# Where the arguments of the levels' decays are computed: two GpSimd subtractions and one exponential, or one VectorE subtraction and two exponentials

## Chip, core and metric

The kernel runs on one core of a Trainium2 chip. The metric is the device time of one launch in microseconds (us). Engines are named as the profile names them: PE (TensorE matmul), PEld (TensorE weight load), DVE (VectorE), ACT (ScalarE), POOL (GpSimd), SP (SyncE).

## What is computed

The kernel is one transformer block on a sequence of 1024 rows of 1024: a modulated norm, one input projection, sparse attention (a top-k of index scores masks the keys), gated linear attention (GLA), an output projection and a gated feed-forward. The change touches the GLA alone:

```python
def step(S, inp):                       # one chunk of 64 rows, all heads
    qc, kc, vc, gc = inp
    b = jnp.cumsum(gc, axis=2)          # running sum of the log decays
    diff = b[:, :, :, None, :] - b[:, :, None, :, :]
    decay = jnp.exp(jnp.where(tril[None, None, :, :, None], diff, -jnp.inf))
    A = jnp.einsum('bhid,bhjd,bhijd->bhij', qc, kc, decay)
    o = (jnp.einsum('bhij,bhjv->bhiv', A, vc)
         + jnp.einsum('bhid,bhdv->bhiv', qc * jnp.exp(b), S))
    ...
```

## The kernel before

The kernel does not form the three-index `decay`. It takes chunks of 128 rows and splits the triangle of each into seven levels, with half blocks of s = 64, 32, 16, 8, 4, 2 and 1 rows (`LEVELS`). In a block of 2s columns the running sum at column s - 1 is the reference point: the first s columns (keys) are weighted by exp((ref - b)/16), the last s (queries) by exp((b - ref)/16), so that a product of a weighted key and a weighted query carries the right decay. Heads are handled in two pairs, p = 0 and p = 1, with 64 partitions for each head.

`gla_pair(p, ...)` is a generator. At its step n it emits, in this order:

- `masked(n-3)`: two VectorE predicated copies of the products into the triangle `AT` (L819);
- `products(n-2)`: sixteen matmuls in eight groups of two (L810), on the weighted keys and the weighted queries;
- `decayed(n-1)`: four VectorE multiplications of queries by E into `qz` (L799), one GpSimd multiplication of the first halves of E by the keys, in place (L804);
- `decays(n)`: the weights E of level n, a tile of 128x1024 in the ring `gs` of four buffers. Two GpSimd subtractions write the first halves (L790) and the last halves (L791) of all blocks, one ScalarE exponential goes over all of E (L792).

Two more background streams run at the same time: `topk_act` (32 rounds; each has three ScalarE sign passes with a sum, L654, and four small VectorE instructions, L656 to L661) and `topk_dve` (32 rounds; three VectorE counting passes, L625, and two small VectorE instructions, L629 and L631). Main stream are the projections: PE chains of 24 matmuls (L243 to L245, L252 to L254), whose weights are split into two parts by L215, L217, L219 and L220, on POOL, DVE or ACT. After each unit of a projection, `pump` emits one step of a GLA stream where its rate says so, then a round of `topk_act`, then one of `topk_dve`.

`pin()` fixes the order of all PE and of all VectorE instructions of this stretch to the order in which they are emitted. ACT and POOL have no such order: a list scheduler orders their queues at build time, and may place an instruction far ahead of its place in the text. In the trace the POOL subtractions of pair 0's first four levels stand at 153 to 164 us, and those of pair 1's first four at 243 to 257 us, 25 us and 85 us ahead of the multiplications that use them.

Of the kernel before, what the change touches and what calls it, by code (L numbers as in the profile page):

```python
# [14 lines left out]
AF = mybir.ActivationFunctionType  # L15
ALU = mybir.AluOpType

P = 128
# [50 lines left out]
def hymba_block_kernel(  # L69
# [44 lines left out]
    def gs(shape, dt=F32):  # L114
        return g(shape, dt, tag="gs", bufs=NGS)
# [10 lines left out]
    V, A, G, T, S = nc.vector, nc.scalar, nc.gpsimd, nc.tensor, nc.sync  # L126
# [646 lines left out]
    def gla_pair(p, gq, gk, gv, bT):  # L773
# [8 lines left out]
        def decays(lv):  # L782

            s = LEVELS[lv]
            NB = L // (2 * s)
            E = Es[lv] = gs([P, L])
            Ev = E.rearrange("p (a b) -> p a b", b=2 * s)
            bv = bT.rearrange("p (a b) -> p a b", b=2 * s)
            ref = bv[:, :, s - 1:s].to_broadcast([P, NB, s])
            G.tensor_tensor(Ev[:, :, :s], ref, bv[:, :, :s], ALU.subtract)  # L790
            G.tensor_tensor(Ev[:, :, s:], bv[:, :, s:], ref, ALU.subtract)  # L791
            A.activation(E, E, AF.Exp, scale=1.0 / 16)  # L792

        def decayed(lv):
            s, E = LEVELS[lv], Es[lv]
# [29 lines left out]
        for n in range(S1 + 3):  # L825
            if n >= 3:
                masked(n - 3)
            if 2 <= n < S1 + 2:
                products(n - 2)
            if 1 <= n < S1 + 1:  # L830
                decayed(n - 1)
            if n < S1:
                decays(n)
            if n == S1:
                kb = gs([P, L])
                V.tensor_tensor(kb.rearrange("p (a b) -> p a b", b=P),
                                b3[:, :, P - 1:P].to_broadcast([P, NT, P]), b3, ALU.subtract)
                A.activation(kb, kb, AF.Exp, scale=1.0 / 16)
            if n == S1 + 1:

                both = gs([P, L])
                G.tensor_tensor(both, gq, gk, ALU.mult)
                G.tensor_tensor(gk, kb, gk, ALU.mult)
                eb = gs([P, L])
                A.activation(eb, bT, AF.Exp, scale=1.0 / 16)
                G.tensor_tensor(gq, eb, gq, ALU.mult)
            if n == S1 + 2:
                V.tensor_copy(el, eb.rearrange("p (a b) -> p a b", b=P)[:, :, P - 1])
                pd = ps()
                for cc in range(NT):  # L850
                    T.matmul(pd[:, 2 * cc:2 * cc + 2], lhsT=both[:, cc * P:(cc + 1) * P], rhs=hsel,
                             start=True, stop=True)
            yield
# [692 lines left out]
```

## Time and profile before

| | us |
|---|---|
| median of 3 timed runs | 1409.28 (1407.75 to 1411.63) |
| profiled execution | 1407.83 |
| span from its first to its last instruction | 1406.1 |
| PE busy | 1319.4 (94%) |
| DVE busy | 915.8 (65%) |
| ACT busy | 586.4 (42%) |
| POOL busy | 445.8 (32%) |
| L790 and L791, POOL, 28 instructions, 147 to 352 us | 34.1 |
| L792, ACT, 14 exponentials | 14.8 |

Shares of the whole span hide that the stages have different limits. The stretch that matters here is from 150 to about 480 us, where both pairs of the GLA and both top-k streams run beside the projections.

### The profile page before, as it was taken

Reading aid. Unit: us, or ns where it says so; the run is one execution under the profiler, and the core shown is the slowest. Engines: PE = TensorE matmul, PEld = TensorE weight load, DVE = VectorE, ACT = ScalarE, POOL = GpSimd, SP = SyncE. Lnnn points to the kernel's source line nnn. Section 1 sums busy time; section 2 is a strip of 40 time slices with the busy share of each in tenths; the row PEclk is TensorE's granted clock in tenths of the full one; section 3 lists DMA queues with packets and bytes.
Section 4 is the critical chain, followed back from the end, with each engine's and each line's share of the span. In section 5 each row is a group of like instructions: output and inputs, shape, how many; then the busy total and the mean of one; then the engine's idle time right before and its main releaser. Section 6 shows DMA issues by size and latency. Waiting matters only on the chain.

```text
span 1406.1 us, 18387 instructions
## 1 busy us (share of the span) xinstructions
PE 1319.4 (94%) x6979; PEld 1104.1 (79%) x6979; DVE 915.8 (65%) x1525; ACT 586.4 (42%) x1064; POOL 445.8 (32%) x393
## 2 busy tenths in 40 slices
PE   5999989599899998899997999999999999999997
PEld 3777877488788977688886787878888878888886
DVE  3578799758987855875478676654444556576524
ACT  3376655658363235346573333332323325112202
POOL 3560533313310111304222444443444425232101
PEclk9999999799999999999999999999999999999999
DMA  9701010210311344751221233322221346254102
GB/s 267 210 15 31 1 31 30 61 31 16 105 25 38 90 139 149 261 170 31 105 91 53 97 120 120 120 75 90 76 90 64 127 153 223 90 168 150 46 15 105
DMA packets 93630, 136.36 MB, mean 97 GB/s; under 512 B 6403, under 2 KB 72038, under 8 KB 93542
## 3 DMA queue, kind: packets, MB, share of 16 engines
q1 hardware_dynamic: 89576, 121.49, 27.0%
q0 software_dynamic: 3808, 13.64, 3.1%
q8 instruction: 55, 0.90, 0.3%
q14 instruction: 33, 0.27, 0.1%
q10 hardware_dynamic: 158, 0.06, 0.0%
HBM read 111.04 MB, written 24.13 MB: 96 GB/s over the span
## 4 chain that ended last, share of the span: by engine, by line
PE 68%; DVE 16%; issue 5%; DMA 3%; ACT 3%; SPq 2%; POOL 2%; DVEq 0%; ACTq 0%; POOLq 0%
PE pw L1280 5%; PE pw L1281 4%; PE pw L1282 4%; PE ps L1280 4%; PE ps L1282 4%; PE ps L1281 4%; PE pw L1486 3%; PE pw L1487 3%; PE ps L1486 3%; PE ps L1487 3%; PE pw L1488 3%; PE ps L1488 3%; DVE junk_d L625 3%; PE ps L252 2%; PE ps L253 2%
## 5 line engine op out<-in xcount | busy, mean ns | idle before, releaser
L654 ACT ACTIVATE junk_a<-g,Ya 128x1024 int8<-128x1024 f32 (+2 forms) x96 | 99.9, 1041 | 50.5 <-DVE Ya L661 47.8
L252 PE MATMUL ps<-whi,g 128*128 128x256 f32 x384 | 113.1, 295 | 3.3 <-DVE whi L217 1.4
L254 PE MATMUL ps<-wlo,g 128*128 128x256 f32 x384 | 110.5, 288 | 0.7 <-DVE wlo L220 0.7
L253 PE MATMUL ps<-whi,g 128*128 128x256 f32 x384 | 110.5, 288 | 0.0
L1311 POOL TENSOR_TENSOR g<-g,h 128x512 f32<-128x512 f32 x33 | 52.2, 1582 | 138.2 <-issue 54.0
L1452 POOL TENSOR_TENSOR raw<-raw,g 128x1024 f32<-128x1024 f32 x22 | 58.5, 2665 | 110.2 <-DMA raw<-in_w_down_dram 105.3
L245 PE MATMUL ps<-g,wlo 128*128 128x512 f32 x208 | 82.5, 397 | 5.3 <-DVE wlo L220 5.3
L243 PE MATMUL ps<-g,whi 128*128 128x512 f32 x208 | 84.0, 404 | 0.0
L244 PE MATMUL ps<-g,whi 128*128 128x512 f32 x208 | 82.3, 396 | 0.0
L1282 PE MATMUL ps<-g,wlo 128*128 128x512 f32 x192 | 75.7, 394 | 6.3 <-DVE wlo L1273 6.2
L252 PEld LDWEIGHTS ps<-whi,g 128*128 128x128 f32 x384 | 75.6, 197 | 6.4 <-issue 3.5
L1280 PE MATMUL pw<-g,whi 128*128 128x512 f32 x192 | 76.9, 401 | 1.5 <-DVE h L1329 1.5
L1280 PE MATMUL ps<-g,wlo 128*128 128x512 f32 x192 | 75.7, 394 | 0.7 <-ACT g L1185 0.7
L254 PEld LDWEIGHTS ps<-wlo,g 128*128 128x128 f32 x384 | 75.6, 197 | 0.9 <-DVE wlo L220 0.9
L253 PEld LDWEIGHTS ps<-whi,g 128*128 128x128 f32 x384 | 75.7, 197 | 0.0
L1281 PE MATMUL ps<-g,wlo 128*128 128x512 f32 x192 | 75.3, 392 | 0.4 <-DVE g L1186 0.4
L1281 PE MATMUL pw<-g,whi 128*128 128x512 f32 x192 | 74.9, 390 | 0.0
L1282 PE MATMUL pw<-g,whi 128*128 128x512 f32 x192 | 74.8, 389 | 0.0
L625 DVE TENSOR_SCALAR_CACHE_REDUCE junk_d<-g,Zd 128x640 bf16<-128x640 f32 (+5 forms) x96 | 71.4, 744 | 2.4
L1249 POOL TENSOR_TENSOR gs<-raw,raw 128x512 f32<-128x512 f32 x19 | 25.1, 1319 | 119.5 <-DMA raw<-in_w_gate_up_dram 82.6
L1273 DVE TENSOR_TENSOR wlo<-gs,wlo 128x512 fp32r<-128x512 f32 x44 | 39.6, 901 | 29.0 <-ACT wlo L1272 28.5
L1273 DVE TENSOR_TENSOR whi<-gs,whi 128x512 fp32r<-128x512 f32 x44 | 38.7, 879 | 28.8 <-ACT whi L1272 28.3
(408 smaller groups left out, 3871.0 us busy)
## 6 DMA issues: line engine op xcount, KB each, us to landing
raw<-in_w_gate_up_dram SPq DMA_DIRECT2D x42, 512.0 KB, 3.6
g<-in_w_mod_dram SPq DMA_DIRECT2D x24, 512.0 KB, 6.8
raw<-in_w_in_dram SPq DMA_DIRECT2D x24, 512.0 KB, 3.9
whi<-in_w_mod_dram POOLq DMA_DIRECT2D x24, 512.0 KB, 4.7
hid_d<-g SPq DMA_DIRECT2D x22, 512.0 KB, 2.9
raw<-in_w_down_dram SPq DMA_DIRECT2D x22, 512.0 KB, 4.2
gs<-hid_d SPq DMA_DIRECT2D x22, 512.0 KB, 3.4
g<-in_x_dram SPq DMA_DIRECT2D x16, 512.0 KB, 4.5
```

The source lines that it names most:

```text
L243: T.matmul(pt, lhsT=wh, rhs=rh, start=(k == 0), stop=False)
L252: T.matmul(pt, lhsT=rh, rhs=wh, start=(k == 0), stop=False)
L253: T.matmul(pt, lhsT=rl, rhs=wh, start=False, stop=False)
L254: T.matmul(pt, lhsT=rh, rhs=wl, start=False, stop=(k == KC - 1))
L625: V.tensor_scalar(junk_d[:, :W], top[t] if 0 < i < 16 else score[t], Z[:, j:j + 1].bitcast(F32), -float(TOPK), ALU.is_ge, ALU.add, accum_o ...
L654: A.activation(junk_a[:, :W], score[t], AF.Sign, bias=Y[:, j:j + 1].bitcast(F32), accum_out=acc[:, j:j + 1])
L1280: T.matmul(pt, lhsT=w[:, 0, kk, :], rhs=rh, start=(not more and kk == 0), stop=False, skip_group_check=more)
L1281: T.matmul(pt, lhsT=w[:, 0, kk, :], rhs=rl, start=False, stop=False, skip_group_check=more)
L1282: T.matmul(pt, lhsT=w[:, 1, kk, :], rhs=rh, start=False, stop=(kk == 3), skip_group_check=more)
L1486: T.matmul(po[m], lhsT=ah[:, r], rhs=wh[:, cc], start=(f == 0), stop=False)
L1487: T.matmul(po[m], lhsT=al[:, r], rhs=wh[:, cc], start=False, stop=False)
L1488: T.matmul(po[m], lhsT=ah[:, r], rhs=wl[:, cc], start=False, stop=(f == len(cur) - 1))
```

## The change

The subtractions move from GpSimd to VectorE and become one instruction over the whole of E, with b - ref in both halves. The first halves then have the opposite sign, so that the exponential is split into two, with scale -1/16 on the first halves and 1/16 on the last halves.

```diff
             bv = bT.rearrange("p (a b) -> p a b", b=2 * s)
-            ref = bv[:, :, s - 1:s].to_broadcast([P, NB, s])
-            G.tensor_tensor(Ev[:, :, :s], ref, bv[:, :, :s], ALU.subtract)
-            G.tensor_tensor(Ev[:, :, s:], bv[:, :, s:], ref, ALU.subtract)
-            A.activation(E, E, AF.Exp, scale=1.0 / 16)
+            V.tensor_tensor(Ev, bv, bv[:, :, s - 1:s].to_broadcast([P, NB, 2 * s]), ALU.subtract)
+            A.activation(Ev[:, :, :s], Ev[:, :, :s], AF.Exp, scale=-1.0 / 16)
+            A.activation(Ev[:, :, s:], Ev[:, :, s:], AF.Exp, scale=1.0 / 16)
```

## Rows read from the trace of the kernel before

**Rows 1.** The page's 40 slices of 35 us: busy tenths of PE, granted clock in tenths.

```profile
PE   5999989599899998899997999999999999999997
PEclk9999999799999999999999999999999999999999
```

**Rows 2.** Four stretches: length, then busy us (count) by engine, granted clock, DMA.

```profile
167.00:216.00 49.00, 44.01 (x295) 39.62 (x293) 45.65 (x108) 27.29 (x52) 19.13 (x15) 0.97 0.10 28
243.00:279.00 36.00, 20.89 (x93) 17.04 (x91) 30.36 (x73) 23.14 (x39) 13.75 (x13) 0.81 0.19 58
326.00:346.00 20.00, 17.05 (x145) 16.89 (x144) 18.72 (x47) 18.89 (x31) 6.63 (x6) 1.00 0.01 2
346.00:403.00 57.00, 49.18 (x324) 45.69 (x324) 54.23 (x122) 27.86 (x49) 16.49 (x10) 0.91 0.21 65
```

**Rows 3.** Timeline of PE: start, us, instruction, idle time before it and its releaser.

```profile
250.14 0.80 PE L245 MATMUL ps<-g,wlo 128*128 128x512 f32 x1 [5.29 <-DVE wlo L220]
...
279.35 0.77 PE L875 MATMUL pw<-diag,g 64*128 64x128 f32 x2 [6.74 <-DVE diag L888]
...
345.54 1.13 PE L810 MATMUL pw<-h,gs 128*128 128x128 f32 x8 [2.94 <-DVE h L799]
```

**Rows 4.** Groups by line: count, busy us, mean ns, idle before and its releasers.

```profile
L791 POOL TENSOR_TENSOR gs<-g 128x512 f32<-128x512 f32 x14 | 18.0, 1287 | 0.0
L790 POOL TENSOR_TENSOR gs<-g 128x512 f32<-128x512 f32 x14 | 16.1, 1152 | 90.3 <-DVE g L567 52.4 <-PE pw L810 27.7 <-DVE acca L656 10.2
L792 ACT ACTIVATE gs<-gs 128x1024 f32<-128x1024 f32 x14 | 14.8, 1054 | 19.8 <-POOL gs L791 8.7 <-DVE Fa L659 7.0 <-DVE Ya L661 4.1
```

**Rows 5.** Timeline of DVE: a 128x1024 subtraction and the instruction behind it.

```profile
381.81 1.23 DVE L836 TENSOR_TENSOR gs<-g 128x1024 f32<-128x1024 f32 x1
382.95 2.37 DVE L656 TENSOR_TENSOR acca<-acca,need 128x3 f32<-128x3 f32 x1
```

**Rows 6.** Timeline of DVE: one free group (178.66); the others beside POOL's subtractions.

```profile
150.17 8.85 DVE L567 SCALAR_TENSOR_TENSOR g<-gs,wcol,g 128x1024 f32<-128x1024 f32 x5
...
178.66 1.73 DVE L799 TENSOR_TENSOR h<-g,gs 64x256 f32<-64x256 f32 x4
...
183.45 0.82 DVE L629 TENSOR_SCALAR md<-acc 128x3 int32<-128x3 f32 x1
...
200.73 4.31 DVE L799 TENSOR_TENSOR h<-g,gs 64x256 f32<-64x256 f32 x4
...
243.25 1.05 DVE L657 TENSOR_SCALAR ma<-acca 128x3 int32<-128x3 int32 x1
...
253.70 1.03 DVE L661 SCALAR_TENSOR_TENSOR Ya<-ma,Ya 128x3 int32<-128x3 int32 x1
...
339.12 1.20 DVE L631 SCALAR_TENSOR_TENSOR Zd<-md,Zd 128x3 int32<-128x3 int32 x1
...
342.87 4.14 DVE L799 TENSOR_TENSOR h<-g,gs 64x256 f32<-64x256 f32 x4
```

**Rows 7.** Timelines of ACT (two rows) and DVE: the top-k's wait for its sign passes.

```profile
163.09 0.56 ACT L337 COPY g<-ps 128x512 f32<-128x512 f32 x1
...
164.70 1.04 ACT L792 ACTIVATE gs<-gs 128x1024 f32<-128x1024 f32 x1
...
167.86 0.16 DVE L656 TENSOR_TENSOR acca<-acca,need 128x3 f32<-128x3 f32 x1 [7.74 <-ACT junk_a L654]
...
260.48 0.16 DVE L656 TENSOR_TENSOR acca<-acca,need 128x3 f32<-128x3 f32 x1 [3.02 <-ACT junk_a L654]
```

**Rows 8.** All instructions of a line: duration ns min/median/max, first and last start.

```profile
L804 POOL TENSOR_TENSOR gs<-gs,g x14: 1266/1290/2187, 168.4 to 352.5; 128x512 f32<-128x512 f32 x14
L625 DVE TENSOR_SCALAR_CACHE_REDUCE junk_d<-g,Zd x96: 611/746/876, 170.1 to 428.4; 128x640 bf16<-128x640 f32 x17, 128x512 bf16<-128x512 f32 x17, 128x384 bf16<-128x384 f32 x17, 128x640 bf16<-128x640 bf16 x15
```

**Rows 9.** Timeline of DVE ahead of pair 1's first levels.

```profile
318.85 0.16 DVE L656 TENSOR_TENSOR acca<-acca,need 128x3 f32<-128x3 f32 x1 [0.80 <-ACT junk_a L654]
...
324.88 0.16 DVE L656 TENSOR_TENSOR acca<-acca,need 128x3 f32<-128x3 f32 x1 [1.08 <-ACT junk_a L654]
```

## Prediction

> **What bounds the kernel now.** I read the slices first. PE is nearly full throughout, and where it is not, between 140 and 420 us, its clock dips too: the eighth slice has PE at 5 and the clock at 7 [rows 1]. That is where both pairs of the GLA run. Then the busy time by stretch. From 167 to 216 us PE lacks 5.0 us (49.00 - 44.01), from 243 to 279 us 15.1, from 326 to 346 us 2.95 and from 346 to 403 us 7.8 [rows 2]: 31 us of idle PE. DVE is 93 to 95% busy in three of the four. Between these stretches, at 216 to 243 and from 279 to 326 us, PE hardly waits. Last, what ended PE's idle times: the three long ones, 5.29, 6.74 and 2.94 us, all ended with a DVE instruction, and these are a weight split, a copy of the GLA's state and the weighted queries [rows 3]. They are late only because DVE's order is fixed and each stands behind rounds of the two top-k streams. So in these four stretches DVE's one long queue sets the end, and a microsecond more or less in it goes to the end nearly whole. Elsewhere PE does, and DVE's time is free.
>
> **What the change adds to DVE.** Fourteen subtractions of 128x1024. The row nearest to one is the kernel's own subtraction with a broadcast operand of that size: it takes 1.23 us, and the next starts 1.14 us after it [rows 5]. 14 x 1.14 = 16.0. The place is fixed by the pin: behind `decayed(n-1)`, ahead of the round of `topk_act`. Pair 0's seven stand at about 173 to 215 us, all in the full queue. Of pair 1's, the first levels meet DVE waits of 0.80 and 1.08 us [rows 9], which hide 1.9. Added to the path: 16.0 - 1.9 = +14.1. The two ends are 0 hidden and four levels hidden (+16.0 and +11.4).
>
> **What it takes from POOL, and by that from DVE.** POOL loses 28 instructions, 34.1 us [rows 4]. POOL is not on the path and its own time is worth nothing. But DVE is held up while they run. A free group of four L799 takes 1.73 us; beside POOL's subtractions one took 4.31 and another 4.14. Three-element instructions, 0.16 to 0.17 us when free, took 0.82 to 1.20 us [rows 6]. I went through all DVE instructions from 140 to 480 us that took over 0.15 us more than the same form when free, and put each excess to the POOL instruction whose span covers its start. L790 and L791 own 15.4 us in twenty of them:
> - 150 to 160 us, 2.8, in the five L567 that took 8.85 us together and the instruction behind them [rows 6]. Worth nothing: DVE then waits 7.74 us anyway [rows 7];
> - 183 to 205 us, 4.6 (from the row at 183.45 to that at 200.73, whose excess of 2.6 is 1.1 due to L804);
> - 243 to 247 us, 2.5 (three like the row at 243.25);
> - 252 to 255 us, 1.65 (two, the last at 253.70);
> - 338 to 347 us, 3.75 (0.4, 1.04 at 339.12, 0.87, and 1.5 of the 2.4 in the group at 342.87) [rows 6].
> Off the path: -12.5.
>
> **What moves with it: L804.** Fourteen multiplications on POOL stay, 1.29 us each [rows 8]. Today they cost DVE 10.0 us by the same count. Each will now follow its own subtraction by one exponential, and behind most subtractions stand four small instructions (0.7 us), then three L625 (2.2 us), which no POOL instruction lengthened: their longest is 0.876 us, the free time of the 640-column form [rows 8]. So many of them will meet nothing. Ends: none meets DVE (-10), or all do at today's 1.1 for each that does (+5.4). I take -4, between the middle and the end that the order on DVE speaks for. The Trainium skill says why L625 is left alone (SBUF — State Buffer, section "Who interferes with whom"): VectorE and GpSimd share one port pair, an instruction of VectorE with two SBUF inputs locks against a GpSimd instruction that reads SBUF, whoever comes first holds it for the whole instruction, and a `tensor_scalar` that writes out its accumulator is not among the takers. The rows agree with it on L567, L799 and L625. Taken as strict it would make this term about -8 and the sum -8.8; it would also let the new subtraction, with two SBUF inputs, hold up L804.
>
> **What moves on ACT.** The exponential of 1.05 us [rows 4] becomes two of half the columns. No row has that form; the ends are 0.53 (half of 1.05) and 1.05 each, and the nearest 128x512 instruction is the copy of 0.56 [rows 7]; I take 0.6, so 1.2 a level, 2 us more in all. ACT has that much free (27 of 49 us busy from 167 to 216 [rows 2]). The order counts more. Today the exponential of pair 0's fourth level stands between sign passes of the first round, 164.70, and DVE waits for that round [rows 7]; gone, that is -1.0. I don't count the whole wait of 7.74: the passes stand behind the copy at 163.09, which waits for PE's matmuls, and that copy stays where it is [rows 7]. Likewise two of pair 1's exponentials, run early, delay the round before 260.48 (a wait of 3.02); gone, I take -1.9, since DVE arrives 1.65 us earlier and the round needs its 3.2 us (from the end of the copy, 163.65, to 167.86, less the exponential [rows 7]). Sum -2.9.
>
> **The new wait.** E(n) must now pass DVE, then ACT, before `decayed(n)` on DVE; POOL used to be up to 85 us ahead. A subtraction waits for its buffer of E (PE's products four levels back, over 10 us earlier) and so does not hold DVE. `decayed(n)` waits for the last half's exponential. Between the two stand one round of each top-k stream (3.6 us) at most levels, and a split and a predicated copy (2.4 us) at the tightest, against 1.2 for both exponentials and 0.2 for the signals. If one sign pass (a third of the 3.2) gets in between, 2.5. What is queued behind a late `decayed(n)` is the whole of DVE's order, and PE's products. I take +1.5 for all levels; the ends are 0 and 7 (0.5 a level).
>
> **Clock.** From 243 to 279 us the granted clock averaged 0.81, part of it at the lower level, right behind the idle time of 5.29 us [rows 2, 3]. With shorter gaps PE may keep the upper one. At full clock its 20.89 us would be 16.9, so the ends are 0 and -4; DVE sets that stretch, so I take -1.
>
> **Sum.** 14.1 - 12.5 - 4 - 2.9 + 1.5 - 1 = -4.8 us. The profiled execution took 1407.83 us, of which 1.7 lie outside its span of 1406.1; it is 1.45 below the median of 1409.28. All terms are differences inside the span, so I set the sum against the median: 1409.28 - 4.8 = 1404.5. By stage: pair 0 gains about 7, mostly after 243 us, where only the removals lie; pair 1 loses about 2, as its seven subtractions (less 1.9) and seven instead of three L804 come into a stretch that gives back 3.75.
>
> **Rivals.** (1) A wash, 1409 (1405 to 1413). DVE's relief at 243 to 279 us only lets it run into ACT's loop: a round of sign passes takes ACT 3.2 us, and DVE already waits for it in places (0.80, 1.08 and 3.02 us [rows 7, 9]). Then half of pair 0's gain goes, and L804 meets DVE as often as today. For it: ACT's passes are serial. Against it: ACT idles 22 of 49 us from 167 to 216. Worked out: -4.8 + 3 + 2 = 0 or so, 1409.3.
> (2) Slower, 1418. ACT's queue is filled at build time. If an exponential stands there ahead of the round of sign passes that could have run before it, ACT waits for DVE's subtraction, and DVE then waits for the exponentials and the passes: 1.2 + 3.2 = 4.4 us a level. From a second such level on the gain is gone; with three it is -4.8 + 13.2 = +8.4, 1418. For it: today's queue has exponentials between passes [rows 7], and DVE waited 3.02 us for that. Against it: the passes of a round depend on the round before, which is ahead of the subtraction on DVE by 5 us or more, so that they are ready first. A held-up L804 (the longest today took 2.19 us, free ones 1.27 [rows 8]) would come on top, since late weighted keys hold PE's products.
> (3) A larger gain, 1397. If the first round's passes come ahead of the copy at 163.09, the wait of 7.74 shrinks by up to 6.4 us, and L804 meets DVE nowhere: -4.8 - 3 - 4 = -12. Against it: two queue orders must fall right.
> That the subtraction does not stay in its place on DVE is excluded by the pin.
>
> **Chances.** Forecast (1401 to 1407.5) 0.45, (1) 0.28, (2) 0.19, (3) 0.08. The forecast holds two thirds of its weight below 1405.05, which is 0.3% (4.2 us) under the median, about what a measurement of this kernel can tell from no change. Faster: 0.30 + 0.05 of (1) + 0.08 + a little from the unknown bounds = 0.46. Slower: 0.17 of (2) and 0.04 of (1), 0.21. Same: 0.33. The range for 8 in 10 leaves out most of (2)'s upper half and (3)'s lower: 1396.5 to 1416.
>
> **What would show it.** DVE busy from 150 to 410 us about unchanged although it has 14 instructions more; no instruction of 0.17 us lengthened to 0.8 to 1.2 at 243 to 255 us; PE's gap at 250 us about half, that at 279 us under 4 us; L804 beside L625 most of the time. Wrong, if L799 shows new idle time ahead of it released by ACT, if L656 waits for L654 more often than in the places shown, or if the new subtraction takes more than 1.25 us.

## The result, and the profile after

| | before | after |
|---|---|---|
| median | 1408.51 us (1407.00 to 1411.63, 4 runs) | 1399.18 us (1398.80 to 1401.24, 4 runs) |
| ratio | | 0.9932, 95% interval 0.9920 to 0.9944 |
| profiled execution, span | 1407.83, 1406.1 us | 1398.97, 1397.2 us |

The change takes 9.3 us (0.68%) off, where the forecast was 4.8. The direction was right and the size was half: the time lies below the forecast's own 1401 to 1407.5 us and inside its range for 8 in 10, 1396.5 to 1416. In what follows, "before" and "after" stand for the two kernels. How the gain came about is in good part not what the forecast said, as the stages show.

The page of after: busy time by engine, then PE and its granted clock in 40 slices, to set beside [rows 1].

```profile
PE 1308.9 (94%) x6979; PEld 1095.5 (78%) x6979; DVE 906.9 (65%) x1539; ACT 588.3 (42%) x1078; POOL 413.8 (30%) x365
...
PE   5899999797799998899998999999999999999997
...
PEclk9999999899999999999999999999999999999999
```

DVE has 14 instructions more and is busy 8.9 us less (915.8 before): what it no longer loses beside GpSimd is more than what it got. PE's idle time over the span is not smaller: 1406.1 - 1319.4 = 86.7 us before, 1397.2 - 1308.9 = 88.3 after. PE's busy time is 10.5 us smaller with the same 6979 matmuls. So a look at PE's idle time alone would have found nothing; the stretches have to be looked at one by one, and at the clock.

Three stretches of before, then the same three of after (length, busy us and count by engine, granted clock, DMA):

```profile
150.00:235.00 85.00, 80.01 (x483) 70.55 (x482) 73.75 (x145) 51.32 (x83) 39.78 (x27) 0.98 0.09 26
235.00:326.00 91.00, 75.54 (x467) 65.85 (x466) 64.34 (x176) 52.99 (x119) 27.14 (x20) 0.89 0.14 41
326.00:403.00 77.00, 66.23 (x467) 62.59 (x466) 72.95 (x168) 46.75 (x79) 23.12 (x15) 0.93 0.16 49
```

```profile
150.00:235.00 85.00, 85.00 (x530) 75.72 (x529) 77.83 (x173) 55.73 (x97) 22.28 (x14) 1.00 0.09 26
235.00:326.00 91.00, 78.66 (x553) 70.50 (x551) 62.83 (x189) 60.12 (x133) 16.34 (x11) 0.94 0.14 42
326.00:403.00 77.00, 60.77 (x396) 55.85 (x397) 71.28 (x164) 44.37 (x80) 22.93 (x11) 0.91 0.18 55
```

In the first stretch PE is now full, 85.00 of 85.00 us at full clock. In the second it does 553 matmuls instead of 467. In the third it does fewer, 396 instead of 467, partly since other work has moved into these times. What is lost there is clearer from pairing. PE's order is pinned and the same in both kernels, so the n-th matmul of one is the n-th of the other; the difference of their starts says how far after is ahead (negative) at that piece of work. At these times of the kernel before:

| work at, us | 150 | 200 | 220 to 240 | 280 | 340 | 400 | 420 to 480 | 1350 |
|---|---|---|---|---|---|---|---|---|
| after, us | -1.5 | -6.3 | -9.4 | -18.9 | -19.3 | -11.4 | -11.1 | -8.9 |

Up to 240 us, where pair 0 runs, 7.9 us are gained (the 1.5 us at 150 us lie ahead of the change's work; the kernels below are there between 0.2 us behind and 2.9 us ahead, so this is scatter between executions). Two kernels below that leave pair 0 as it was (pair 1 alone, and pair 1 later on GpSimd) gain 1.2 us in this stretch too, so about that much of the 7.9 belongs to the one profiled execution of before. From 240 to 280 us another 9.5 us follow, where only the removal of pair 1's early GpSimd work lies. Where pair 1 itself runs, 340 to 420 us, 8.2 us are lost. Behind it 2 us more go, in work that the change does not touch.

### The profile page after: what moved, and what is told of

The parts are those of the page before. It is cut to its first block, busy times and chain, and to the rows that moved or that the text cites. A ratio compares the mean times of both kernels' runs of the same rounds, so it can differ in the third digit from the quotient of the medians.

```text
span 1397.2 us, 18382 instructions
## 1 busy us (share of the span) xinstructions
PE 1308.9 (94%) x6979; PEld 1095.5 (78%) x6979; DVE 906.9 (65%) x1539; ACT 588.3 (42%) x1078; POOL 413.8 (30%) x365
## 4 chain that ended last, share of the span: by engine, by line
PE 63%; DVE 18%; issue 5%; ACT 5%; DMA 3%; POOL 3%; SPq 2%; DVEq 0%; POOLq 0%; ACTq 0%
PE pw L1279 5%; PE pw L1280 4%; PE pw L1281 4%; PE ps L1279 4%; PE ps L1281 4%; PE ps L1280 4%; DVE junk_d L625 3%; PE ps L1486 3%; PE ps L1485 3%; PE ps L1487 3%; PE pw L1486 3%; PE pw L1487 3%; PE pw L1485 3%; ACT junk_a L654 2%; DVE h L798 2%
## 5 line engine op out<-in xcount | busy, mean ns | idle before, releaser
L654 ACT ACTIVATE junk_a<-g,Ya 128x1024 int8<-128x1024 f32 (+2 forms) x96 | 99.9, 1041 | 36.2 <-DVE Ya L661 30.4
L252 PE MATMUL ps<-whi,g 128*128 128x256 f32 x384 | 111.5, 290 | 0.0
L253 PE MATMUL ps<-whi,g 128*128 128x256 f32 x384 | 109.1, 284 | 0.0
L252 PEld LDWEIGHTS ps<-whi,g 128*128 128x128 f32 x384 | 74.2, 193 | 2.7 <-issue 2.0
L253 PEld LDWEIGHTS ps<-whi,g 128*128 128x128 f32 x384 | 74.2, 193 | 0.0
L625 DVE TENSOR_SCALAR_CACHE_REDUCE junk_d<-g,Zd 128x640 bf16<-128x640 f32 (+5 forms) x96 | 71.4, 744 | 2.4
```

The source lines that it names most:

```text
L252: T.matmul(pt, lhsT=rh, rhs=wh, start=(k == 0), stop=False)
L253: T.matmul(pt, lhsT=rl, rhs=wh, start=False, stop=False)
L625: V.tensor_scalar(junk_d[:, :W], top[t] if 0 < i < 16 else score[t], Z[:, j:j + 1].bitcast(F32), -float(TOPK), ALU.is_ge, ALU.add, accum_o ...
L654: A.activation(junk_a[:, :W], score[t], AF.Sign, bias=Y[:, j:j + 1].bitcast(F32), accum_out=acc[:, j:j + 1])
```

## Experiments

The questions: which pair brings the gain; whether it is the head start of the first top-k round, the freed VectorE, or merely the order on ACT; what the added subtractions cost; and whether engine, form or place of the subtractions matters. The expectations name the theories as they stood before each kernel ran. "Ahead" is the paired lead over the kernel before, as in the table above; times are medians, with the ratio to the kernel before and its interval.

### One pair at a time

The changed three lines stand under a condition, the old four lines in the other branch:

```diff
+            if p == 0:                     # e2_pair1: p == 1
                 V.tensor_tensor(Ev, bv, bv[:, :, s - 1:s].to_broadcast([P, NB, 2 * s]), ALU.subtract)
```

Pair 0 alone:

> Only pair 0's subtractions move to VectorE; pair 1's stay on GpSimd, two instructions and one exponential a level. Theory A (the gain of the change is pair 0's: ScalarE's queue no longer waits for GpSimd ahead of the first top-k round, about 6.7 us, and pair 1's own stretch only loses, about 8 us): 1398 to 1402 us, the first round's L656 near 160 us, and no loss behind 300 us; what stays of before is the damage that pair 1's early instructions do at 243 to 257 us. Theory B (the gain is VectorE's relief from the shared port alone, equal in kind for both pairs): seven subtractions cost 8 us and give back 4.6 to 7.5, so 1408 to 1411 us.

1400.65 us, 0.9949 (0.9934 to 0.9964). It is 0.6 us ahead at 150 us, 8.5 at 220, 9.6 at 280 and still 9.6 at 480.

Pair 1 alone:

> Only pair 1's subtractions move to VectorE. Theory A: the first round of the top-k starts as late as before (near 168 us), 243 to 279 us gains 8 to 10 us since pair 1's early GpSimd subtractions and exponentials are gone from there, and the stretch from 305 to 400 us loses 7 to 9: 1405 to 1410 us. Theory B: 1404 to 1407 us with no stretch that loses over 3 us.

1408.98 us, 1.0008 (0.9991 to 1.0025). It is 2.7 us ahead at 240 us, 10.9 at 280, 10.3 at 340, 1.9 at 400 and 3.6 at 480. So the two halves do different things: pair 0's is worth 7 us and keeps them; pair 1's gains 8.2 us between 240 and 280 us and loses 8.4 of its own between 340 and 400, 6.7 if 480 is taken for the end. By the medians it is a wash.

### Only the order on ACT

On the kernel before, pair 0's exponentials are queued behind the last sign pass of the first top-k round, so that nothing stands ahead of that round (`first_round[0]` is that pass). GpSimd keeps the subtractions.

```diff
-            A.activation(E, E, AF.Exp, scale=1.0 / 16)
+            with tc.issue_after(first_round[0].ins) if p == 0 else nullcontext():
+                A.activation(E, E, AF.Exp, scale=1.0 / 16)
```

> The kernel before, with one change in ScalarE's queue: pair 0's exponentials are issued behind the last sign pass of the first top-k round. All subtractions stay on GpSimd. Theory A: the first round's L656 comes at 160 to 163 us and not at 168, and 5 to 7 us of it last to the end: 1401 to 1405 us. Theory B: VectorE's lock decides, which this leaves as it is: 1407 to 1410 us.

1407.74 us, 0.9994 (0.9982 to 1.0006): nothing. Its trace shows why. First ACT in the kernel before (start, us, instruction, idle time before it and its releaser; the copy and the exponential of [rows 7] lie between the last two lines and behind them):

```profile
155.99 1.06 ACT L792 ACTIVATE gs<-gs 128x1024 f32<-128x1024 f32 x1 [1.15 <-POOL gs L791]
160.00 1.06 ACT L792 ACTIVATE gs<-gs 128x1024 f32<-128x1024 f32 x1 [2.95 <-POOL gs L791]
162.12 1.06 ACT L792 ACTIVATE gs<-gs 128x1024 f32<-128x1024 f32 x1 [1.06 <-POOL gs L791]
...
163.55 1.15 ACT L654 ACTIVATE junk_a<-g,Ya 128x1024 int8<-128x1024 f32 x1
```

and in after:

```profile
155.90 1.15 ACT L654 ACTIVATE junk_a<-g,Ya 128x1024 int8<-128x1024 f32 x1 [3.82 <-DVE g L568]
...
157.05 0.57 ACT L337 COPY g<-ps 128x512 f32<-128x512 f32 x1
157.52 1.04 ACT L654 ACTIVATE junk_a<-g,Ya 128x896 int8<-128x896 f32 x1
```

The first sign pass needs DVE's L568. In before it is built into ACT's queue behind three exponentials, which wait for GpSimd, and starts at 163.55, though L568 ended at 160.1. In after it starts as L568 releases it. The DVE side, after first and then the reordered kernel:

```profile
148.71 6.83 DVE L567 SCALAR_TENSOR_TENSOR g<-gs,wcol,g 128x1024 f32<-128x1024 f32 x5
...
159.74 0.16 DVE L656 TENSOR_TENSOR acca<-acca,need 128x3 f32<-128x3 f32 x1 [3.88 <-ACT junk_a L654]
```

```profile
149.56 8.86 DVE L567 SCALAR_TENSOR_TENSOR g<-gs,wcol,g 128x1024 f32<-128x1024 f32 x5
158.45 1.05 DVE L568 TENSOR_TENSOR g<-g,dmin 128x128 f32<-128x128 f32 x1
163.38 0.24 DVE L660 TENSOR_TENSOR acca<-acca,need 128x3 f32<-128x3 f32 x1 [3.88 <-ACT junk_a L656]
163.65 0.99 DVE L661 TENSOR_SCALAR ma<-acca 128x3 int32<-128x3 int32 x1
```

The new order alone brings the first round's wait from 7.74 [rows 7] to the same 3.88 us as in after, and its first small instruction from 167.86 to 163.38. But L567 is still held up beside GpSimd (8.86 against 6.83 for five), and GpSimd's work now meets the first rounds, whose small instructions take 1 us instead of 0.17. By the third round 0.5 us of the 4.5 is left. So the head start did not last while GpSimd's work on the same levels stayed beside DVE.

### Engine or form

The kernel after with its one subtraction on GpSimd: the change's form without its engine.

```diff
-            V.tensor_tensor(Ev, bv, bv[:, :, s - 1:s].to_broadcast([P, NB, 2 * s]), ALU.subtract)
+            G.tensor_tensor(Ev, bv, bv[:, :, s - 1:s].to_broadcast([P, NB, 2 * s]), ALU.subtract)
```

> The kernel after with its one subtraction of 128x1024 on GpSimd instead of VectorE, so the form of the change (one subtraction, two exponentials of opposite scale) without the change of engine. Theory A (the engine is the point: GpSimd's work in the first round of the top-k stays the same in time, about 2.1 us a level by two rows of 1.04): within 3 us of the kernel before, 1404 to 1411 us, and the first round's VectorE wait for the sign passes over 6 us as in the kernel before. Theory B (fewer and other instructions are the point): most of the change's gain is there, 1398 to 1403 us.

1411.14 us, 1.0016 (1.0003 to 1.0028). All instructions of the line (duration ns min/median/max), and DVE beside the first four of them:

```profile
L789 POOL TENSOR_TENSOR gs<-g x14: 1892/1958/2122, 153.1 to 351.3; 128x1024 f32<-128x1024 f32 x14
```

```profile
150.35 11.99 DVE L567 SCALAR_TENSOR_TENSOR g<-gs,wcol,g 128x1024 f32<-128x1024 f32 x5
...
167.71 0.16 DVE L656 TENSOR_TENSOR acca<-acca,need 128x3 f32<-128x3 f32 x1 [5.04 <-ACT junk_a L654]
```

One GpSimd instruction takes about as long as the two (1.96 us), holds L567 up more (11.99 us for five), and the first round is as late as before. So the change's form without its engine does not pay; the old form on VectorE was not tried. That the wait is 5.04 us and not over 6, as expected, is because DVE itself comes later by 2.5 us.

### Which of pair 0's levels

The same condition as above, with `p == 0 and lv < 4` and with `p == 0 and lv >= 4`.

> Only the first four levels of pair 0 move to VectorE, those whose GpSimd subtractions ran ahead of the first top-k round. Theory A (most of pair 0's gain is that early bundle, on GpSimd, on the port and in ScalarE's queue): the first L656 at 160 to 161 us, 4 to 8 us gained by 220 us, 1401 to 1405 us. Theory B (the relief at 183 to 205 us, levels 4 to 6, carries it): under 3 us gained by 220 us, 1405 to 1408 us.

1404.84 us, 0.9979 (0.9968 to 0.9990).

> Only the last three levels of pair 0 move to VectorE. Theory A: the first L656 stays near 167 us; 4.6 us of VectorE's waits go, 3.4 us of subtractions come: 0 to 2 us gained by 220 us, 1406 to 1409 us. Theory B: 4 to 7 us gained by 220 us, 1401 to 1404 us.

1404.76 us, 0.9982 (0.9972 to 0.9991). The first four levels are 5.8 us ahead at 200 us and 4.7 at 220; the last three, 1.6 and 4.6. Each gives about half of pair 0's 8.5 us (by the ratios 3.0 and 2.5 us, where pair 0 alone has 7.2). The last three's time lies between the two that were expected. My theory, that the head start at the first levels makes pair 0's gain, is only half right: the last three levels have no head start and gain as much, in the stretch from 183 to 205 us where [rows 6] has GpSimd holding DVE up.

### What the added subtractions cost

The kernel after with the subtraction cut to one column. It leaves the subtraction out: the exponentials read the running sum itself.

```diff
-            V.tensor_tensor(Ev, bv, bv[:, :, s - 1:s].to_broadcast([P, NB, 2 * s]), ALU.subtract)
-            A.activation(Ev[:, :, :s], Ev[:, :, :s], AF.Exp, scale=-1.0 / 16)
-            A.activation(Ev[:, :, s:], Ev[:, :, s:], AF.Exp, scale=1.0 / 16)
+            V.tensor_tensor(E[:, 0:1], bT[:, 0:1], bT[:, 0:1], ALU.subtract)
+            A.activation(Ev[:, :, :s], bv[:, :, :s], AF.Exp, scale=1.0 / 16)
+            A.activation(Ev[:, :, s:], bv[:, :, s:], AF.Exp, scale=1.0 / 16)
```

> The changed kernel with the VectorE subtraction cut to one column, so that its order and its waits stay; the exponentials read the running sums themselves, which leaves the subtraction out. VectorE loses 14 x 1.06 = 14.8 us. If VectorE's queue is the bound in both pairs' stretches, 10 to 14 us come off: 1385 to 1390 us, and the loss from 305 to 400 us shrinks from 8 to about 2. If the loss there comes from ScalarE's queue order and not from VectorE's load, 1391 to 1396 us with the loss there still over 5.

1398.34 us, 0.9940 (0.9920 to 0.9959), no different from after within the intervals, and slower than either expected range (1385 to 1390, 1391 to 1396). And the kernel after with each of pair 0's subtractions done twice:

```diff
+            for _ in range(2 if p == 0 else 1):
                 V.tensor_tensor(Ev, bv, bv[:, :, s - 1:s].to_broadcast([P, NB, 2 * s]), ALU.subtract)
```

> The changed kernel with each of pair 0's seven subtractions done twice on VectorE, 8.0 us more. If VectorE's queue is the bound in pair 0's stretch, 7 to 9 us slower than the changed kernel: 1406 to 1408 us. If PE is the bound there by now and VectorE has a lead of some us, as the run with one-column subtractions makes likely (it took 7.4 us out of that stretch and gained nothing by 300 us), 0 to 5 us slower: 1399 to 1404 us.

1410.90 us, 1.0024 (1.0011 to 1.0038). Against after that is some 12 us for 8 us of DVE work, and slower than either expected range. By the pairing it turns the lead at 220 us from 9.4 us ahead to 3.9 behind. The stretch from 150 to 235 us, first with the short subtraction and then with the doubled one:

```profile
150.00:235.00 85.00, 85.00 (x530) 75.64 (x528) 71.88 (x170) 55.68 (x96) 23.11 (x14) 1.00 0.09 26
```

```profile
150.00:235.00 85.00, 78.12 (x465) 67.87 (x464) 77.85 (x158) 51.49 (x88) 17.94 (x13) 0.94 0.08 26
```

With the short one DVE is busy 6 us less than in after, and PE does the same 530 matmuls: it was full already. What DVE saves, it waits: 1.62 us twice for ACT's passes and 2.88 us for PE, where after has no such waits. With the doubled one DVE is as busy as in after (77.85 and 77.83), it just gets less far, and PE does 65 matmuls fewer, at a clock of 0.94. So after stands at the crossing of two limits in pair 0's stretch: less DVE work buys nothing, more of it is paid in full, and above its price when PE falls idle and its clock falls as well. PE's longest gap there stands ahead of L759, whose operand DVE writes; in the kernel before it was 0.55 us:

```profile
213.47 3.75 PE L759 MATMUL pw<-g,wg 16*128 16x512 f32 x4 [5.14 <-DVE g L819]
```

In pair 1's stretch the short subtraction does help: this kernel is 18.6 us ahead at 340 us and 17.4 at 480, so it loses 1.2 us there where after loses 8.2. So by one execution of each kernel 7.0 us of pair 1's loss are the seven subtractions on a DVE that sets the end (7 x 1.14 = 8.0 in the forecast's terms). The medians do not confirm it: the whole kernel is only 1 us faster than after by the medians, although its profiled execution is 6.3 us ahead at 480 us. Why is not settled. That execution took 1394.86, the fastest of its four, 3.5 us under their median, and 4.1 us of its lead go behind 480 us.

### Another place on GpSimd

If pair 1's gain at 240 to 280 us comes only from GpSimd's early work being gone there, it needs no DVE. In the first kernel pair 0 goes as in after and pair 1 stays on GpSimd, its subtractions queued behind GpSimd's last weight split; in the second one pair 0 stays on GpSimd too, where it was.

```diff
+            if p == 0:
                 V.tensor_tensor(Ev, bv, bv[:, :, s - 1:s].to_broadcast([P, NB, 2 * s]), ALU.subtract)
...
+            else:
+                ref = bv[:, :, s - 1:s].to_broadcast([P, NB, s])
+                with tc.issue_after(last_split[0].ins):
+                    G.tensor_tensor(Ev[:, :, :s], ref, bv[:, :, :s], ALU.subtract)
+                    G.tensor_tensor(Ev[:, :, s:], bv[:, :, s:], ref, ALU.subtract)
+                A.activation(E, E, AF.Exp, scale=1.0 / 16)
```

> Pair 0's subtractions on VectorE as in the changed kernel; pair 1's stay on GpSimd, but are queued there behind the last weight split that GpSimd does ahead of them, so that they stand near 265 to 310 us, where PE is the bound. Theory A (pair 1's early GpSimd instructions at 243 to 257 us cost pair 0's stretch 8 to 9 us, its VectorE subtractions cost its own stretch 7 to 8, and each is needed for neither): matmuls near 300 us come 17 to 19 us earlier than before, and no more than 2 us of that are lost by 420 us: 1389 to 1393 us. Theory B (the two are the price of the work wherever it stands): 1398 to 1402 us, as with pair 0 alone.

1392.07 us (1390.73 to 1396.93, 5 runs), 0.9899 (0.9882 to 0.9917), faster than after, whose interval (0.9920 to 0.9944) lies wholly above this one. GpSimd's timeline:

```profile
258.28 5.00 POOL L221 TENSOR_TENSOR wlo<-raw,whi 128x1024 fp32r<-128x1024 f32 x2 [29.42 <-DVE whi L218]
263.22 1.06 POOL L799 TENSOR_TENSOR gs<-g 128x512 f32<-128x512 f32 x1
264.22 1.08 POOL L800 TENSOR_TENSOR gs<-g 128x512 f32<-128x512 f32 x1
```

> The kernel before with one thing changed: pair 1's GpSimd subtractions are queued behind the last GpSimd split of a weight instead of where they stood, at 243 to 255 us. Pair 0 is as before, nothing is on VectorE. Theory A (pair 1's early GpSimd work and the exponentials behind it cost some 8 us between 243 and 279 us, and their place is what costs, not their engine): the difference of e5_mix and e1_pair0, 8.6 us, comes off the kernel before, 1397 to 1402 us, and the lead of 7 to 10 us appears between 240 and 280 us of the trace and stays. Theory B (it pays only together with pair 0's move): 1405 to 1409 us.

1403.39 us, 0.9959 (0.9942 to 0.9976). Ahead by:

| work at, us | 240 | 280 | 340 | 480 | 1350 |
|---|---|---|---|---|---|
| pair 0 on DVE, pair 1 later on GpSimd | -10.7 | -20.3 | -17.5 | -17.8 | -17.1 |
| pair 1 later on GpSimd, nothing else | -1.8 | -10.0 | -7.3 | -7.7 | -4.8 |

Three kernels, pair 1 on DVE and pair 1 later on GpSimd with and without pair 0, gain 8.2, 9.5 and 8.2 us from 240 to 280 us. What they share is that the subtractions, and the exponentials behind them, are gone from 243 to 257 us, and with them the multiplications at 261 us. So the old place cost 8 to 9 us, and both other places that were tried cure it. Which part weighs how much was not tried; the rows of before and after give 4.1 us of DVE's instructions that the subtractions lengthened, 2.2 that the multiplications did, and 2.1 less of DVE's waits for ACT (3.02 and 1.29 us in before, 1.21 and 0.96 in after). But only the later place on GpSimd keeps it: some 3 us are lost around 310 us and nothing at 340 to 480, where pair 1 on DVE loses 8. GpSimd's subtractions still lengthen DVE's instructions there, by 7.1 us in the first kernel by the forecast's count, but no more than those 3 us show in PE's matmuls. In the last kernel 5.8 us by the ratio is left, between the two theories' times. The trace has the lead of theory A; 2.9 us of it go behind 480 us.

The parts add up: pair 0 on DVE (-7.2 by its ratio) and pair 1 later (-5.8) are -13.0, and both together measured -14.2.

## Why the prediction was right in sign and half in size

The changed instructions in after (duration ns min/median/max, first and last start):

```profile
L789 DVE TENSOR_TENSOR gs<-g x14: 1218/1225/1227, 165.9 to 357.4; 128x1024 f32<-128x1024 f32 x14
...
L790 ACT ACTIVATE gs<-gs x14: 629/632/670, 167.2 to 358.7; 128x512 f32<-128x512 f32 x14
...
L791 ACT ACTIVATE gs<-gs x14: 612/616/672, 167.7 to 359.3; 128x512 f32<-128x512 f32 x14
...
L803 POOL TENSOR_TENSOR gs<-gs,g x14: 1271/1347/3700, 167.9 to 359.4; 128x512 f32<-128x512 f32 x14
```

**Prices.** The subtraction takes 1.22 us, 1.13 to 1.15 to the next instruction; the forecast had 1.23 and 1.14. The half exponentials take 0.61 to 0.63, forecast 0.6. The Trainium skill (ScalarE: Activation LUTs, section "What ACT_TABLE_LOAD costs") gives 186 ns and 0.833 ns an element for an activation with immediate scale and bias, by which an estimate is 186 + 512 x 0.833 = 613 ns. The rows agree (medians of 616 and 632 ns).

**"A microsecond more or less in DVE's queue goes to the end nearly whole", and by that +14.1.** The price holds, up to a limit that the forecast did not have. An estimate by stage from the rows of both traces (the subtractions at 1.14 us, what GpSimd lengthens on DVE by the forecast's count, DVE's waits for ACT) makes DVE's queue 7.5 us shorter up to 240 us, 8.4 shorter from 240 to 280 and 8.8 longer behind it; the pairing has 7.9, 9.5 and 8.2. So both pairs' subtractions were paid nearly in full. Nothing of the 1.9 was hidden: the waits of 0.80 and 1.08 us are there in after too, ahead of pair 1's first subtraction. The limit is PE. In pair 0's stretch it had 85.00 - 80.01 = 4.99 us of idle time to give back, and gave all of it: PE is full there in after. With 2.9 us less PE time for the same 481 matmuls, by the pairing, that makes the 7.9 us gained. Past this, less DVE time buys nothing, as the short subtraction showed; more of it is paid, as the doubled one showed. So the sum needed a cap there: PE's idle time and what its matmuls can save. The change just reached it, and the cap is not what made the gain larger than forecast.

**-12.5 for GpSimd's lengthening of DVE.** The mechanism held: of the 15.4 us due to L790 and L791 nothing is left, and no small instruction of DVE between 243 and 255 us is longer than 0.17. Its ledger was wrong at one place: the 2.8 us at L567 and L568, "worth nothing" because DVE waits 7.74 us anyway, are on the path once that wait shrinks, since ACT's first pass is released by L568.

**-4 for L804.** It measured -7.0 us: the multiplications (L803 in after) now lengthen four DVE instructions by 3.0 in all, where it was nine by 10.0. Ten of the fourteen lengthen nothing. L625 still takes 611 to 875 ns. The rule of the Trainium skill (SBUF — State Buffer, section "Who interferes with whom") that a `tensor_scalar` that writes out its accumulator is not among the takers was the better guide here (about -8 by the forecast's estimate).

**-2.9 for ACT's order.** This is the step that failed most. The failed reading is the copy at 163.09 [rows 7]. I took it to wait for PE's matmuls, and the passes behind it with it. It followed the exponential ahead of it in ACT's queue without a gap, and the exponentials waited for GpSimd; in after, with PE 1.5 us ahead, the same copy runs at 157.05. The first round came 8.1 us earlier: 1.5 was there already, 2.8 is L567 and L568, and 3.9 is the wait, 7.74 to 3.88. So -1.0 should have been -6.7 with the 2.8. This is the third rival's mechanism, which I gave 0.08; its time (1397) was nearer than the forecast's. Order alone did not pay, as the reordered kernel shows.

**+1.5 for the new wait.** L798 (L799 in before) waited for ACT once, 1.5 us. The second rival's mechanism, an exponential ahead of a sign pass, came once in pair 1. ACT and then DVE in after:

```profile
321.29 0.63 ACT L790 ACTIVATE gs<-gs 128x512 f32<-128x512 f32 x1 [1.78 <-DVE gs L789]
...
322.34 0.92 ACT L654 ACTIVATE junk_a<-g,Ya 128x768 int8<-128x768 f32 x1
```

```profile
320.02 1.23 DVE L789 TENSOR_TENSOR gs<-g 128x1024 f32<-128x1024 f32 x1
323.39 0.90 DVE L656 TENSOR_TENSOR acca<-acca,need 128x3 f32<-128x3 f32 x1 [2.13 <-ACT junk_a L654]
...
361.55 1.77 DVE L629 TENSOR_SCALAR md<-acc 128x3 int32<-128x3 f32 x1
363.36 2.27 DVE L631 SCALAR_TENSOR_TENSOR Zd<-md,Zd 128x3 int32<-128x3 int32 x1
```

ACT waited 1.78 us for the subtraction with a ready pass behind it, and DVE 2.13 us for that pass. That is one level, half of what the rival's price of 4.4 said; it did not come a second time. In all, DVE's waits for ACT in the work from 280 to 420 us grew from 5.3 to 8.6 us, where the forecast had 1.5 for all levels. The last two rows are DVE beside GpSimd's L220 and L841, 3.7 us more than their free times together. Meetings of DVE with GpSimd's other work, which no term of the forecast has, cost 2.9 us more in the same work than in before.

**-1 for the clock.** From 150 to 480 us the stretches at the lower level, 1.2 GHz, add up to 34.1 us before and 23.9 after. At half speed 10.2 us of them are worth up to 5 us, which is a bound, since PE also idles in them. From 235 to 326 us the granted clock went from 0.89 to 0.94. The forecast's ends were 0 and -4. The stretch that it spoke of came out at the far end: the 91 matmuls from 243 to 279 us took PE 20.8 us in before and 17.0 in after.

**By stage.** Pair 0 was to gain 7, mostly after 243 us. It gained 7.9 before 240, and the removals after it 9.5. Pair 1 was to lose 2; it lost 8.2. That two errors of 6 to 8 us partly cancel is luck: the total lies nearer to the forecast than its parts. In the forecast's terms, as measured: +16.0 for the subtractions, -15.4 and -7.0 for what GpSimd's subtractions and multiplications no longer lengthen, +2.0 for its other work beside DVE and -2.7 for DVE's waits for ACT make an estimate of -7.1 us. The pairing has -9.6 from 150 to 480 us; the rest is of the size of what PE's matmuls saved, and was not separated further.

**The signs named.** DVE's busy time about unchanged: 211.04 and 211.94 us from 150 to 403. PE's gaps in after (those over 1.5 us from 200 to 400 us):

```profile
237.17 0.50 PE L245 MATMUL ps<-g,wlo 128*128 128x512 f32 x1 [1.68 <-DVE wlo L220]
...
260.43 0.77 PE L874 MATMUL pw<-diag,g 64*128 64x128 f32 x2 [7.50 <-DVE diag L887]
...
330.18 3.12 PE L809 MATMUL pw<-h,gs 128*128 128x128 f32 x13 [6.88 <-DVE h L798]
...
341.32 1.35 PE L809 MATMUL pw<-h,gs 128*128 128x128 f32 x10 [1.71 <-DVE h L798]
...
356.61 0.57 PE L809 MATMUL pw<-h,gs 128*128 128x128 f32 x3 [2.96 <-DVE h L798]
...
368.87 1.41 PE L809 MATMUL pw<-h,gs 128*128 128x128 f32 x5 [7.38 <-DVE h L798]
```

The gap at 250 us [rows 3] shrank from 5.29 to 1.68, more than half. The one at 279 was to fall under 4 and grew from 6.74 to 7.50; it is the same work, 18.9 us earlier. The first rival is not the reason: DVE's waits for ACT's passes on the way there got shorter (1.21 and 0.96 us, from 3.02 and 1.29). PE's idle time over those 91 matmuls fell from 15.5 to 9.6 us in all, and PE now waits for most of it at one place. One sign of being wrong came, the idle time ahead of L799 that ACT released (1.5 us, once); L656 waited more than 0.2 us for L654 in 10 places, as before. The two gaps ahead of L809 at 330 and 369 us show pair 1's loss: PE waits for weighted queries behind DVE's longer order.

**Left open.** 2 us of after's lead, and 2 to 5 us of that of several other kernels, go between 480 and 1350 us, in work that no kernel touches. PE's idle time there is the same in before and after, 22.53 us, and its matmuls take the 2.2 us more. The lower clock takes up 6.8 us there in before and in the kernel with pair 0 on DVE and pair 1 later on GpSimd, and their matmuls take 847.6 and 847.8 us; it takes 10.2 or 13.7 us in after and all others, and their matmuls take 849.5 to 852.2. Whether that is chance was not tried.

## What to carry to other kernels

Work of an idle engine is not free: look at what its instructions lengthen on the engine that sets the end, and at which queue they hold through an instruction that waits for them. Before taking such relief at its full size, cap it stage by stage with the idle time of the engine that would bound next, and what its own work can save (here 4.99 and 2.9 us). Where two halves of a change lie in different stages, try each alone and then another place for the one that doesn't pay: here that made 1392 us of 1399.

## What the runs showed of the hardware that was not expected

- A held-up DVE and a held-up GpSimd cost each other: GpSimd's subtraction of 128x512 takes 1.04 us alone and up to 2.07 beside L567, whose five take 6.83 us without it, 8.85 beside two levels' subtractions in two instructions each, and 11.99 beside three levels' in one each: 1.0 and 1.7 us a level. The Trainium skill (SBUF — State Buffer, section "Who interferes with whom") has the rule that an instruction of VectorE with two SBUF inputs locks against a GpSimd instruction that reads SBUF; the rows agree, and show that the longer GpSimd instruction was the worse neighbour for the same work.
- The new subtraction has two SBUF inputs, and none of the fourteen was lengthened (1218 to 1227 ns). The multiplication on GpSimd that took 3.70 us instead of 1.27 ran beside two weight splits on VectorE (L220), not beside a subtraction.
- An instruction of 128x3 on DVE, 0.16 us when free, took up to 2.37 us beside GpSimd [rows 5].
